# Layer norms of a two-block network: moved onto token rows on VectorE, ahead of the TensorE transposes

## The chip, the core and the metric

The kernel runs on one core of one Trainium2 chip. The metric is the device time of one launch in microseconds (us); a run is compared by the median over several launches.

## What is computed

One launch runs two transformer-like blocks on 512 tokens of width 1024, in fp32. The first ends in a mixture of experts (MoE) and a norm by `final_g`. The second has two layers, and it holds five layer norms: one at its entry, two in each layer.

```python
def layer_norm(x, g, b):
    xf = x.astype(jnp.float32)
    mu = jnp.mean(xf, -1, keepdims=True)
    var = jnp.mean(jnp.square(xf - mu), -1, keepdims=True)
    return ((xf - mu) * lax.rsqrt(var + LN_EPS) * g.astype(jnp.float32) + b.astype(jnp.float32)).astype(x.dtype)

def second_block(x, ...):
    x = layer_norm(x, ln_in_g, ln_in_b)
    for l in range(DEPTH_2):
        proj = jnp.einsum('bsd,de->bse', x, w_in[l])
        ...
        mix = jnp.einsum('bse,ed->bsd', merged, w_out[l])
        x = layer_norm(DN_ALPHA * x + mix, ln1_g[l], ln1_b[l])
        gu = jnp.einsum('bsd,df->bsf', x, w_ffn_in[l])
        hidden = jax.nn.silu(gu[..., :D_FF]) * gu[..., D_FF:]
        ffn = jnp.einsum('bsf,fd->bsd', hidden, w_ffn_out[l])
        x = layer_norm(DN_ALPHA * x + ffn, ln2_g[l], ln2_b[l])
    return x
```

## The kernel before

The 512 tokens are four tiles of 128 rows. A product in fp32 is made of three TensorE matmuls on numbers that are split into a rounded high part and a low part: `split` (lines 138 to 140) lets ScalarE cast the high part (line 139) and VectorE subtract it from the source to get the low part (line 140); `split_sb` (lines 142 to 144) does both on VectorE. Weights are split the same way after they are loaded: their tiles are called `raw` (as loaded), `wh` and `wl` (128 x 1024, sometimes narrower). `mmk` (lines 289 to 295) issues the three matmuls.

A matmul wants its activations with the features on the partitions, so between a layer norm and the next product the token rows have to be transposed. `normalizer` (line 1216) makes the function `norm` for one of the five norms; `turn` inside it is the transposition. For one tile of 128 rows the kernel before does this:

- VectorE collects mean and variance (`bn_stats`, `bn_aggr`), ScalarE takes a reciprocal root (`rsqrt`, line 185), VectorE refines it with three operations on 128 x 1 (lines 190 to 192) and makes the shift -mean * r (line 246).
- ScalarE applies scale and shift to the whole row (line 1232, 128 x 1024, in place).
- TensorE transposes the eight 128 x 128 pieces into two PSUM banks called `xt`, four to a bank (line 1246).
- For each piece ScalarE applies gain and bias, which are now per partition, from PSUM into an SBUF tile `xs` (line 1249), casts it into the high half of a page `xT` (line 139), and VectorE subtracts to make the low half (line 140).
- GpSimd applies the gain row `gR` (`lng` in the profile) and the bias row `bR` (`lnb`) to the token rows (lines 1251 and 1252, 128 x 1024 each), which SyncE's queue (SP) then stores for the residual of the next stage (line 1253).

The last norm of the second layer needs no transposition. There ScalarE does scale and shift in two halves of 512 (line 1227), GpSimd applies gain and bias for the first three tiles and VectorE for the last one (lines 1228 and 1229), and each half is stored at once (line 1230).

The five norms will be called stages: A is the one at the entry of the second block (after the MoE, loop from line 1940), B and C are the first and second norm of layer 0, D the first of layer 1, E the last. In B to E the function `residual` (line 1893) runs the product ahead of the norm in two halves of 512 columns; at the end of the second half VectorE adds each tile's PSUM result to the residual (`ev`, line 1905), and the norm follows. `lagging` puts off each `turn` by one tile. After B and D the product with `w_ffn_in` follows (TensorE results called `fm`), after A and C the projection `nav`. The order of the instructions on each engine is set by the framework's scheduler from the program; PSUM has three banks for transposes.

`row` (line 977) loads a 1024-wide vector onto all partitions by a DMA of 512 KB on SP's queue; the gain and bias rows of stage A are asked for behind the last expert weights (`w2r`, line 1403). `columns` (line 165) gathers per-partition vectors by small DMAs on ScalarE's queue and one transpose.

Of the kernel before, what the change touches and what calls it, by code (L numbers as in the profile page):

```python
# [14 lines left out]
AF = mybir.ActivationFunctionType  # L15
OP = mybir.AluOpType
# [48 lines left out]
def build(ctx, tc, I, out, dbg=None):  # L65
    nc = tc.nc
    V, S, G, PE = nc.vector, nc.scalar, nc.gpsimd, nc.tensor
# [8 lines left out]
    def t_(shape, dt, tag, name):  # L76
        uid[0] += 1
        return sb.tile(shape, dt, tag=tag, bufs=NB[tag], name=f"{name}_{uid[0]}")

    def pg(name, dt=F32R, shape=(128, 2, 512)):  # L80
        return t_(list(shape), dt, "PG", name)
# [34 lines left out]
    def sg(name, w=512, dt=F32):  # L116
        return t_([128, w], dt, "SG", name)
# [4 lines left out]
    def sm(name, w, dt=F32):  # L122
        return t_([128, w], dt, "SM", name)
# [5 lines left out]
    def trp(name):  # L129
        return mmp(name, "tr")  # L130

    def const(name, shape, dt=F32):
        return cp.tile(list(shape), dt, name=name)

    def f(ap):
        return ap.bitcast(F32)

    def split(hi, lo, src, eng=None):
        S.copy(hi, src)  # L139
        (eng or V).tensor_tensor(lo, src, f(hi), OP.subtract)  # L140

    def split_sb(hi, lo, src):
# [10 lines left out]
    R1 = [("norm1_g", I["norm1_g"][0], 8), ("b_mod", I["b_mod"][0, 0:2048], 16),  # L153
          ("conv_w", I["conv_w"][0], 40), ("conv_b", I["conv_b"][0], 10), ("b_rg_a", I["b_rg_a"][0], 10),
          ("b_rg_x", I["b_rg_x"][0], 10), ("lam", I["lru_lambda"][0], 10), ("kvg", I["kv_norm_g"][0], 2)]
    R2 = [("ln_in_g", I["ln_in_g_2"], 8), ("ln_in_b", I["ln_in_b_2"], 8), ("ln1_g", I["ln1_g_2"], 16),
          ("ln1_b", I["ln1_b_2"], 16), ("ln2_g", I["ln2_g_2"][0], 8), ("ln2_b", I["ln2_b_2"][0], 8),
          ("b_gate", I["b_gate_2"], 48), ("subln", I["diff_subln_g_2"], 2), ("qng", I["mla_q_norm_g_2"], 6),
          ("kvng", I["mla_kv_norm_g_2"], 4)]
    col = {}  # L160

# [3 lines left out]
    def columns(specs, tag):  # L165
        rows = t_([128, 128], F32, "SG", f"rows{tag}")
        n = 0
        for name, ap, k in specs:
            src = ap.rearrange("(k p) -> k p", p=128) if len(ap.shape) == 1 else \
                ap.rearrange("a (k p) -> (a k) p", p=128)  # L170
            nc.scalar.dma_start(rows[n:n + k, :], src)
            n += k
        ps = trp(f"rowst{tag}")
        PE.transpose(ps[:, 0:n], rows[0:n, :], ident[0:n, 0:n])
        cols = const(f"cols{tag}", [128, n])
        V.tensor_copy(cols, ps[:, 0:n])
        n = 0
        for name, ap, k in specs:
            col[name] = cols[:, n:n + k]
            n += k  # L180
# [1 line left out]
    columns(R0, "0")  # L182


    def rsqrt(v, n):

        y = sm("rsy", n)
        S.activation(y, v, AF.Abs_reciprocal_sqrt)
        t = sm("rst", n)
        V.tensor_tensor(t, y, y, OP.mult)  # L190
        V.scalar_tensor_tensor(t, t, -0.5, v, OP.mult, OP.mult)
        V.scalar_tensor_tensor(t, t, 1.5, y, OP.add, OP.mult)
        return t
# [48 lines left out]
    def ln_stat(mv, v):  # L242

        r = rsqrt(v, 1)
        nm = sm("bnm", 1)
        V.scalar_tensor_tensor(nm, mv[:, 0:1], -1.0, r, OP.mult, OP.mult)
        return r, nm
# [566 lines left out]

    columns(R2, "2")
    rope8 = const("rope8", [128, 2, 4, 8])
# [145 lines left out]
    for d in range(8):  # L962
# [3 lines left out]
        v = sg("mv")  # L966
# [10 lines left out]
    def row(name, src, pinned=False):  # L977
        t = pg(name, F32, (128, 1024))
        ins = load(t, src.partition_broadcast(128))
        if pinned:  # L980
            tc.keep_in_program_order(ins)
        return t
# [230 lines left out]
            V.tensor_tensor(payg[:, :, j, 32 * n:32 * n + 32], oh[:, :, j], bc(f(val)[:, :, j], 32), OP.mult)  # L1213
    gates0()

    def normalizer(gcol, bcol, gvec, bvec, dst):

        gR = row("lng", gvec, True)
        bR = row("lnb", bvec, True)
        pages = []  # L1220

        def norm(i, v, mv, var, later=None):
            r, nm = ln_stat(mv, var)
            if gcol is None:
                eng = V if i == 3 else G
                for cs in (slice(0, 512), slice(512, 1024)):
                    S.activation(v[:, cs], v[:, cs], AF.Identity, bias=nm, scale=r)
                    eng.tensor_tensor(v[:, cs], v[:, cs], gR[:, cs], OP.mult)
                    eng.tensor_tensor(v[:, cs], v[:, cs], bR[:, cs], OP.add)
                    load(dst(i)[:, :, cs], v[:, cs])  # L1230
                return
            S.activation(v, v, AF.Identity, bias=nm, scale=r)
            if later is None:
                turn(i, v)
            else:
                later.append(lambda: turn(i, v))

        def turn(i, v):
            if not pages:
                pages.extend(pg("xT") for _ in range(8))  # L1240
            tk = slice(i * 128, (i + 1) * 128)
            for q in range(2):
                b = trp("xt")
                s = sg("xs")
                for k in range(4):
                    PE.transpose(b[:, k * 128:(k + 1) * 128], v[:, (4 * q + k) * 128:(4 * q + k + 1) * 128], ident)
                for k in range(4):
                    kk, c = 4 * q + k, slice(k * 128, k * 128 + 128)
                    S.activation(s[:, c], b[:, c], AF.Identity, bias=bcol[:, kk:kk + 1], scale=gcol[:, kk:kk + 1])
                    split(pages[kk][:, 0, tk], pages[kk][:, 1, tk], s[:, c])  # L1250
            G.tensor_tensor(v, v, gR, OP.mult)
            G.tensor_tensor(v, v, bR, OP.add)
            load(dst(i), v)

        return norm, pages
# [6 lines left out]
    def rows_of(t):  # L1262
        return lambda i: t[i * 128:(i + 1) * 128, :]
# [100 lines left out]
    def pair_tokens(j):  # L1364
        xg = xgs[j % NG]
        xT = pt_("xx", F32, (128, 8, 128))
        cols = xg.rearrange("p (a j) -> p j a", j=8)
        for q in range(2):
            b = trp("xgt")
            for k in range(4):  # L1370
                PE.transpose(b[:, k * 128:(k + 1) * 128], cols[:, 4 * q + k], ident)
            (V.tensor_copy if q else S.copy)(xT[:, 4 * q:4 * q + 4].rearrange("p k n -> p (k n)"), b)
        return xT
# [6 lines left out]
    def pair_in(j, xT, beside):  # L1380
        pss = []
        for nm in ("moe_w1", "moe_w3"):
            W = [I[nm][0, 2 * j + h].rearrange("(p a) n -> p a n", a=8) for h in range(2)]
            ps = mmp("e1")
            for q in range(4):
                ws = []
                for h in range(2):
                    raw = t_([128, 2, 512], F32, ("PG", "PG", "WH", "WL")[q], "w13")
                    load(raw, W[h][:, 2 * q:2 * q + 2])
                    ws.append(raw)  # L1390
                for k in range(2):
                    both(ps, xT[:, 2 * q + k], [w[:, k] for w in ws], q + k == 0, q + k == 4)
                next(beside, None)
            pss.append(ps)
        return hidden(*pss)
# [25 lines left out]
    def nav_weights(l):  # L1421
        return TM(8, I["w_in_2"][l], 1024, 512, "nav", lead=3)

    g2R = row("g2R", mod_d[3])
    xres = [dr.tile([512, 1024], F32, name=f"xres{n}") for n in range(4)]
# [27 lines left out]
    beside = iter(())  # L1453
# [4 lines left out]
    xs = pair_tokens(0)  # L1458
    for j in range(17):
        hd = None  # L1460
        if j < 16:
            hd = pair_in(j, xs, beside)
        if j < 15:
            xs = pair_tokens(j + 1)
        if j < 14:
            pair_gather(j + 2)
        if j == 16:
            fgR = row("fgR", I["final_g"])
            nav_tm = nav_weights(0).prepare()
        if prev is not None:  # L1470
            for _ in beside:
                pass
            beside = pair_out(j - 1, prev, pair_loads(j - 1))
        prev = hd
# [39 lines left out]
    def layer(l, xT, nav_tm, x_in, x_mid, x_out):  # L1514
# [378 lines left out]
        def residual(xs, W, src, name, norm, nxt=None):  # L1893
# [18 lines left out]
                lagging(tm.run(xs, ev, nxt if hf else None), later)  # L1912
            return tm.next

        norm, xT = normalizer(col["ln1_g"][:, 8 * l:8 * l + 8], col["ln1_b"][:, 8 * l:8 * l + 8], I["ln1_g_2"][l], I["ln1_b_2"][l], rows_of(x_mid))
        residual(mT, I["w_out_2"][l], x_in, "mix2", norm)


# [4 lines left out]
        for j in range(22):  # L1923
            pgt = first.pop(0) if j < 2 else fgt.tile(128 * j)
            s = sg("ffs")
# [4 lines left out]
            p = (pg if j < 16 else pt_)("hid")  # L1930
            split_sb(p[:, 0], p[:, 1], s)
            hid.append(p)
        norm, xT = normalizer(*((col["ln2_g"], col["ln2_b"]) if l == 0 else (None, None)), I["ln2_g_2"][l], I["ln2_b_2"][l], x_out)
        if l == 0:
            return xT, residual(hid, I["w_ffn_out_2"][l], x_mid, "ffo", norm, nxt=lambda: nav_weights(1))
        residual(hid, I["w_ffn_out_2"][l], x_mid, "ffo", norm)

    lat0 = {}
    norm, xT = normalizer(col["ln_in_g"], col["ln_in_b"], I["ln_in_g_2"], I["ln_in_b_2"], rows_of(xres[0]))
    for i in range(4):  # L1940
        a = h1t[i]

# [4 lines left out]
        mv = bn(a, 1024)  # L1947
        v = sm("msq", 1)
# [3 lines left out]
    xT, nav_tm = layer(0, xT, nav_tm, xres[0], xres[1], rows_of(xres[2]))  # L1952
# [32 lines left out]
```

## Time and profile before

| | before |
|---|---|
| median of 3 runs | 3204.37 us (3203.67 to 3213.02) |
| the profiled execution | 3206.89 us |
| its span in the trace | 3205.0 us |
| mean granted TensorE clock | 0.976 of full speed |
| TensorE matmuls (PE) | 2981.3 us, 93% of the span |
| VectorE (DVE) | 1871.9 us, 58% |
| ScalarE (ACT) | 1197.2 us, 37% |
| GpSimd (POOL) | 374.9 us, 12% |

The profile was taken on one execution, whose own time is 1.89 us above its span: that is what lies around the first and last instruction. Busy times add up what an engine works; for an engine that waits for another inside an instruction, the instruction is shown longer. Where a row ends in brackets, they hold the idle time of that engine just before, and what ended it.

### The profile page before, as it was taken

What the parts mean: (1) busy time and instruction counts of PE and PEld (TensorE: products, weight loads), DVE (VectorE), ACT (ScalarE), POOL (GpSimd) and SP (SyncE); (2) the same over time, 40 slices, a digit from 0 to 9 for tenths busy, and PEclk for the clock granted to TensorE, in tenths of its full rate; (3) what the DMA queues carried; (4) which work ended last, traced back from release to release, by engine and by line L of the source; (5) the groups of instructions that cost most, each with busy time, mean ns of one, the idle gap of its engine ahead of it and who ended that gap; (6) DMA issues with size and microseconds to landing.
All of it is one profiled execution on the core that took longest, in us unless ns stands there. A gap on an engine that the chain in (4) does not pass through costs nothing.

```text
span 3205.0 us, 36688 instructions
## 1 busy us (share of the span) xinstructions
PE 2981.3 (93%) x13749; PEld 2213.1 (69%) x13749; DVE 1871.9 (58%) x3485; ACT 1197.2 (37%) x2138; POOL 374.9 (12%) x307
## 2 busy tenths in 40 slices
PE   6988999879999997999999899998999999989998
PEld 5766777733333335888877788887878876778886
DVE  6799887633332337554689744435554589764434
ACT  4555343200000015444567432224444577442222
POOL 2133000200000003111001300002211000220001
PEclk9989999989999998999999999999999999999999
DMA  6232755679999993342234532342433234622342
GB/s 218 91 96 81 235 191 187 219 282 362 377 364 367 377 374 97 125 128 92 71 112 137 193 103 89 105 138 99 144 112 103 68 107 116 220 92 92 105 138 59
DMA packets 296385, 534.21 MB, mean 167 GB/s; under 512 B 30342, under 2 KB 172916, under 8 KB 296198
## 3 DMA queue, kind: packets, MB, share of 16 engines
q1 hardware_dynamic: 293480, 527.46, 47.8%
q0 software_dynamic: 2304, 4.20, 0.5%
q8 instruction: 110, 1.80, 0.2%
q14 instruction: 77, 0.63, 0.1%
q10 hardware_dynamic: 414, 0.12, 0.0%
HBM read 486.54 MB, written 44.38 MB: 166 GB/s over the span
## 4 chain that ended last, share of the span: by engine, by line
PE 63%; DVE 8%; issue 3%; ACT 3%; DMA 1%; POOL 1%; SPq 0%; POOLq 0%; DVEq 0%; ACTq 0%
PE e L1378 12%; PE fm L292 9%; PE fm L295 9%; PE fm L293 9%; PE ffo L295 2%; PE ffo L293 2%; PE ffo L292 2%; DVE xT L140 2%; PE cmb L1308 1%; PE cmb L1309 1%; DVE wl L140 1%; POOL tl L1640 1%; PE mix L292 1%; PE mix L295 1%; PE mix L293 1%
## 5 line engine op out<-in xcount | busy, mean ns | idle before, releaser
L140 DVE TENSOR_TENSOR wl<-raw,wh 128x1024 fp32r<-128x1024 f32 (+3 forms) x403 | 467.8, 1162 | 316.6 <-ACT wh L139 315.3
L139 ACT CAST wh<-raw 128x1024 fp32r<-128x1024 f32 (+3 forms) x403 | 388.7, 966 | 545.4 <-PE fm L295 226.0
L293 PE MATMUL fm<-xT,wl 128*128 128x512 f32 (+1 forms) x1264 | 483.1, 384 | 9.6 <-DVE wl L140 9.6
L292 PE MATMUL fm<-xT,wh 128*128 128x512 f32 (+1 forms) x1264 | 485.0, 386 | 6.0 <-DVE xT L140 3.5
L295 PE MATMUL fm<-xT,wh 128*128 128x512 f32 (+1 forms) x1264 | 302.6, 382 | 0.0
L1378 PE MATMUL e<-w,xx 128*64 128x512 f32 x1024 | 293.7, 605 | 0.0
L293 PEld LDWEIGHTS fm<-xT,wl 128*128 128x128 f32 x1264 | 240.8, 190 | 55.7 <-DVE wl L140 10.6
L292 PEld LDWEIGHTS fm<-xT,wh 128*128 128x128 f32 x1264 | 240.6, 190 | 52.0 <-DVE xT L140 3.9
L295 PEld LDWEIGHTS fm<-xT,wh 128*128 128x128 f32 x1264 | 232.5, 189 | 45.5
L1378 PEld LDWEIGHTS e<-w,xx 128*64 128x64 f32 x1024 | 78.7, 137 | 139.0 <-issue 131.1
L1310 DVE TENSOR_TENSOR h<-h,cmb 128x512 f32<-128x512 f32 x128 | 84.7, 685 | 109.3 <-PE cmb L1309 108.6
L293 PE MATMUL fm<-uT,wl 128*128 128x512 f32 (+1 forms) x360 | 143.9, 400 | 3.8 <-DVE wl L140 3.8
L292 PE MATMUL fm<-uT,wh 128*128 128x512 f32 (+1 forms) x360 | 143.4, 399 | 0.0
L1378 PE MATMUL e<-w2r,hp 128*64 128x512 f32 x512 | 138.7, 599 | 2.0 <-ACT hp L1413 2.0
L292 PE MATMUL ffo<-wl,hid 128*128 128x512 f32 x352 | 137.1, 390 | 0.0
L293 PE MATMUL ffo<-wh,hid 128*128 128x512 f32 x352 | 136.9, 389 | 0.0
L1640 POOL TENSOR_TENSOR tl<-ml,tl 128x512 f32<-128x512 f32 x32 | 47.7, 1497 | 555.1 <-DVE tl L1636 550.4
L1378 PEld LDWEIGHTS e<-w2r,hp 128*64 128x64 f32 x512 | 52.9, 136 | 82.9 <-issue 63.2
L1927 DVE SCALAR_TENSOR_TENSOR ffs<-ffs,fm 128x512 f32<-128x512 f32 x44 | 30.2, 687 | 134.2 <-ACT ffs L1926 134.2
L295 PE MATMUL ffo<-wh,hid 128*128 128x512 f32 x352 | 108.4, 389 | 0.0
L139 ACT CAST yh<-y 128x512 fp32r<-128x512 f32 x32 | 19.8, 618 | 222.3 <-DVE y L1299 222.3
L140 DVE TENSOR_TENSOR xT<-xs,xT 128x128 fp32r<-128x128 f32 x128 | 86.2, 718 | 23.8 <-ACT xT L139 23.8
(612 smaller groups left out, 6101.2 us busy)
## 6 DMA issues: line engine op xcount, KB each, us to landing
w<-in_moe_w_dram SPq DMA_DIRECT2D x256, 512.0 KB
raw<-in_w_in_dram SPq DMA_DIRECT2D x71, 1024.0 KB
w2r<-in_moe_w_dram SPq DMA_DIRECT2D x128, 512.0 KB
raw<-in_w_ffn_in_dram SPq DMA_DIRECT2D x44, 1024.0 KB
raw<-in_w_mod_dram SPq DMA_DIRECT2D x42, 512.0 KB
raw<-in_w_ffn_out_dram SPq DMA_DIRECT2D x20, 1024.0 KB
raw<-in_w_out_dram SPq DMA_DIRECT2D x12, 1024.0 KB
t_d<-bg SPq DMA_DIRECT2D x48, 256.0 KB
```

The source lines that it names most:

```text
L139: S.copy(hi, src)
L140: (eng or V).tensor_tensor(lo, src, f(hi), OP.subtract)
L292: PE.matmul(ps, l[0], r[1], start=start and n == 0, stop=False)
L293: PE.matmul(ps, l[1], r[0], start=False, stop=False)
L295: PE.matmul(ps, l[0], r[0], start=False, stop=stop and n == len(pairs) - 1)
L1308: PE.matmul(ps, pl, yl[:, cs], start=True, stop=False)
L1309: PE.matmul(ps, pl, yh[:, cs], start=False, stop=True)
L1310: V.tensor_tensor(h1[i][m], h1[i][m], ps, OP.add)
L1378: PE.matmul(ps[hs], lhs[:, hs], rhs[h], start=start, stop=stop)
L1640: G.tensor_tensor(th, m, th, OP.add)
L1927: V.scalar_tensor_tensor(s, s, 1.0, pgt, OP.add, OP.mult)
```

## The change

`norm` now works on the token rows in two VectorE passes: `(v - mean) * gR` over 128 x 1024, which is issued beside ScalarE's reciprocal root and needs no r, and then `v * r + bR` in two halves of 512. TensorE transposes the finished rows. ScalarE casts each piece straight from the PSUM bank, and VectorE subtracts straight from it too; `xs`, ScalarE's scale and shift passes (lines 1232, 1227 and 1249), the operation of line 246 and all GpSimd work of the norms are gone. The rows are stored as they are. The six vectors that were needed per partition leave the list of `columns`. The normalizer of stage A is made at the MoE's step 16, ahead of the last expert pair, so that its two row loads stand elsewhere in SP's queue.

```diff
-    R2 = [("ln_in_g", I["ln_in_g_2"], 8), ("ln_in_b", I["ln_in_b_2"], 8), ("ln1_g", I["ln1_g_2"], 16),
-          ("ln1_b", I["ln1_b_2"], 16), ("ln2_g", I["ln2_g_2"][0], 8), ("ln2_b", I["ln2_b_2"][0], 8),
-          ("b_gate", I["b_gate_2"], 48), ("subln", I["diff_subln_g_2"], 2), ("qng", I["mla_q_norm_g_2"], 6),
+    R2 = [("b_gate", I["b_gate_2"], 48), ("subln", I["diff_subln_g_2"], 2), ("qng", I["mla_q_norm_g_2"], 6),
...
-    def rsqrt(v, n):
+    def rsqrt(v, n, beside=None):
         y = sm("rsy", n)
         S.activation(y, v, AF.Abs_reciprocal_sqrt)
+        if beside:
+            beside()
...
         def norm(i, v, mv, var, later=None):
-            r, nm = ln_stat(mv, var)
-            if gcol is None:
-                eng = V if i == 3 else G
-                for cs in (slice(0, 512), slice(512, 1024)):
-                    S.activation(v[:, cs], v[:, cs], AF.Identity, bias=nm, scale=r)
-                    eng.tensor_tensor(v[:, cs], v[:, cs], gR[:, cs], OP.mult)
-                    eng.tensor_tensor(v[:, cs], v[:, cs], bR[:, cs], OP.add)
+            r = rsqrt(var, 1, lambda: V.scalar_tensor_tensor(v, v, mv[:, 0:1], gR, OP.subtract, OP.mult))
+            for cs in (slice(0, 512), slice(512, 1024)):
+                V.scalar_tensor_tensor(v[:, cs], v[:, cs], r, bR[:, cs], OP.mult, OP.add)
+                if not paged:
                     load(dst(i)[:, :, cs], v[:, cs])
+            if not paged:
                 return
-            S.activation(v, v, AF.Identity, bias=nm, scale=r)
...
                 b = trp("xt")
-                s = sg("xs")
...
-                    S.activation(s[:, c], b[:, c], AF.Identity, bias=bcol[:, kk:kk + 1], scale=gcol[:, kk:kk + 1])
-                    split(pages[kk][:, 0, tk], pages[kk][:, 1, tk], s[:, c])
-            G.tensor_tensor(v, v, gR, OP.mult)
-            G.tensor_tensor(v, v, bR, OP.add)
+                    split(pages[kk][:, 0, tk], pages[kk][:, 1, tk], b[:, c])
             load(dst(i), v)
...
         if j == 16:
             fgR = row("fgR", I["final_g"])
+            norm, xT = normalizer(I["ln_in_g_2"], I["ln_in_b_2"], rows_of(xres[0]))
             nav_tm = nav_weights(0).prepare()
```

How the instructions stand now. First ScalarE in stage B, from the first tile's reciprocal root (`rsy`) on; names end in a number that tells one buffer from another, and what an instruction waits for stands in brackets. Before:

```order
L188 ACTIVATE rsy_15022<-bvr_15020 128x1 [waits DVE_49]
L1232 ACTIVATE res_14831<-res_14831,bnm_15028,rst_15024 128x1024 [waits DMAHW4_49,DVE_49]
L1249 ACTIVATE xs_15080<-xt_15079,cols_2957 128x128 [waits PE_49]
L1249 ACTIVATE xs_15080<-xt_15079,cols_2957 128x128
L139 CAST xT_15071<-xs_15080 128x128 [waits Activation_49]
L139 CAST xT_15072<-xs_15080 128x128 [waits Activation_49]
L1249 ACTIVATE xs_15080<-xt_15079,cols_2957 128x128
L188 ACTIVATE rsy_15062<-bvr_15060 128x1 [waits DVE_49]
L1249 ACTIVATE xs_15080<-xt_15079,cols_2957 128x128
```

And with the change:

```order
L186 ACTIVATE rsy_14968<-bvr_14966 128x1 [waits DVE_49]
L139 CAST xT_15017<-xt_15025 128x128 [waits PE_49]
L139 CAST xT_15018<-xt_15025 128x128 [waits DVE_49]
L139 CAST xT_15019<-xt_15025 128x128 [waits DVE_49]
L186 ACTIVATE rsy_15008<-bvr_15006 128x1 [waits DVE_49]
L139 CAST xT_15020<-xt_15025 128x128 [waits DVE_49]
L139 CAST xT_15021<-xt_15038 128x128 [waits PE_49]
L139 CAST xT_15022<-xt_15038 128x128 [waits DVE_49]
L139 CAST xT_15023<-xt_15038 128x128 [waits DVE_49]
L139 CAST xT_15017<-xt_15092 128x128 [waits PE_49]
L139 CAST xT_15021<-xt_15105 128x128 [waits PE_49]
```

The passes of lines 1232 and 1249 are gone; a cast that is not the first of its bank now waits for VectorE (DVE), where it waited only for ScalarE itself before.

VectorE at the same place with the change, for the second tile (`res_14779`), from the addition of its residual to the end of its norm:

```order
L1899 SCALAR_TENSOR_TENSOR res_14779<-res_14779,mix_3209_14977 128x512 [waits PE_49]
L140 TENSOR_TENSOR xT_15017<-xt_15025,xT_15017 128x128 [waits Activation_49]
L216 BN_STATS bst_14909<-res_14779 128x6 [waits DVE_49]
L140 TENSOR_TENSOR xT_15018<-xt_15025,xT_15018 128x128 [waits Activation_49]
L221 BN_AGGR bmv_15004<-bst_14909 128x2 [waits DVE_49]
L1252 TENSOR_SCALAR bvr_15006<-bmv_15004 128x1 [waits DVE_49]
L1223 SCALAR_TENSOR_TENSOR res_14779<-res_14779,bmv_15004,lng_14773 128x1024
L190 TENSOR_TENSOR rst_15011<-rsy_15008 128x1 [waits Activation_49]
L140 TENSOR_TENSOR xT_15019<-xt_15025,xT_15019 128x128
L191 SCALAR_TENSOR_TENSOR rst_15011<-rst_15011,bvr_15006 128x1 [waits DVE_49]
L192 SCALAR_TENSOR_TENSOR rst_15011<-rst_15011,rsy_15008 128x1 [waits DVE_49]
L1225 SCALAR_TENSOR_TENSOR res_14779<-res_14779,rst_15011,lnb_14775 128x512 [waits DVE_49]
```

The two row passes (lines 1223 and 1225) stand among the subtractions of the tile before (line 140), which read the PSUM bank `xt` instead of `xs`.

SP's queue ahead of the last expert pair, with the change (the eight `w2r` loads that follow are shown by their first):

```order
L979 DMA fgR_9345<-in_final_g_dram 128x1024
L979 DMA lng_9347<-in_ln_in_g_dram 128x1024
L979 DMA lnb_9349<-in_ln_in_b_dram 128x1024
L393 DMA raw_9351<-in_w_in_dram 128x4x512
L393 DMA raw_9353<-in_w_in_dram 128x4x512
L1396 DMA w2r_9399<-in_moe_w_dram 128x1024
```

`lng` and `lnb` stood behind the eighth `w2r` load before; now both `raw` loads and all eight `w2r` loads come after them.

## Rows read from the trace of the kernel before

**Rows 1.** Windows, stages A to E: us, busy of PE, PEld, DVE, ACT, POOL, granted clock, DMA share, GB/s.

```profile
1209.40:1262.90 53.50, 35.27 (x128) 26.11 (x129) 41.68 (x79) 31.30 (x84) 21.56 (x10) 0.81 0.18 64
1810.30:1863.00 52.70, 40.44 (x249) 35.78 (x248) 37.22 (x72) 30.00 (x79) 19.81 (x8) 0.90 0.19 70
2189.60:2244.80 55.20, 45.98 (x202) 36.73 (x201) 38.77 (x73) 31.14 (x81) 20.26 (x8) 0.91 0.27 91
2796.10:2848.80 52.70, 40.64 (x249) 36.11 (x249) 37.26 (x72) 30.07 (x79) 19.58 (x8) 0.90 0.19 71
3175.40:3205.00 29.60, 16.27 (x72) 13.14 (x70) 17.77 (x36) 6.89 (x12) 15.26 (x12) 0.84 0.27 71
```

**Rows 2.** VectorE beside GpSimd in stage B: timeline (start us, us, engine, line, operation).

```profile
1819.24 2.39 POOL L1252 TENSOR_TENSOR res<-res,lnb 128x1024 f32<-128x1024 f32 x1
1819.30 2.48 DVE L140 TENSOR_TENSOR xT<-xs,xT 128x128 fp32r<-128x128 f32 x1
1821.70 0.15 DVE L190 TENSOR_TENSOR rst<-rsy 128x1 f32<-128x1 f32 x1
```

**Rows 3.** The subtractions of all norm stages, by tile: duration ns min/median/max.

```profile
L140 DVE TENSOR_TENSOR xT<-xs,xT x128: 229/282/2520, 1217.0 to 2838.3; 128x128 fp32r<-128x128 f32 x128
```

**Rows 4.** The path through stage B: timeline; the last row is the next stage's first.

```profile
1811.07 0.69 DVE L216 BATCH_NORM_STATS2 bst<-res 128x6 f32<-128x512 f32 x1
...
1833.01 1.20 PE L1246 MATMUL xt<-ident,res 128*128 128x128 f32 x8 [2.68 <-ACT res L1232]
...
1837.44 2.83 DVE L140 TENSOR_TENSOR wl<-raw,wh 128x1024 fp32r<-128x1024 f32 x1
...
1840.33 0.58 PE L293 MATMUL fm<-xT,wl 128*128 128x256 f32 x1 [4.31 <-DVE wl L140]
...
1849.13 3.67 DVE L140 TENSOR_TENSOR xT<-xs,xT 128x128 fp32r<-128x128 f32 x7
...
1863.02 0.40 PE L292 MATMUL fm<-xT,wh 128*128 128x512 f32 x1
```

**Rows 5.** Groups of VectorE instructions by shape: busy us, mean ns of one, idle before.

```profile
L140 DVE TENSOR_TENSOR wl<-raw,wh 128x1024 fp32r<-128x1024 f32 x314 | 391.9, 1249 | 299.3 <-ACT wh L139 298.4 <-PE idx L321 0.5
L795 DVE SCALAR_TENSOR_TENSOR macc<-raw,csil,macc 128x1024 f32<-128x1024 f32 x28 | 36.0, 1287 | 5.3 <-DMA raw<-in_w_mod_dram 5.3
L1059 DVE SCALAR_TENSOR_TENSOR u<-u,rst,sh2R 128x512 f32<-128x512 f32 x8 | 5.6, 746 | 0.1
```

**Rows 6.** The end of stage A on VectorE: timeline.

```profile
1250.17 5.62 DVE L140 TENSOR_TENSOR xT<-xs,xT 128x128 fp32r<-128x128 f32 x8 [4.97 <-ACT xT L139]
```

**Rows 7.** The last tile of stage E: timeline.

```profile
3191.71 0.69 DVE L1905 SCALAR_TENSOR_TENSOR res<-res,ffo 128x512 f32<-128x512 f32 x1 [0.62 <-PE ffo L295]
...
3193.59 0.20 ACT L188 ACTIVATE rsy<-bvr 128x1 f32<-128x1 f32 x1 [0.95 <-DVE bvr L1259]
3193.83 0.81 DVE L190 TENSOR_TENSOR rst<-rsy 128x1 f32<-128x1 f32 x1 [0.27 <-ACT rsy L188]
...
3200.14 0.69 DVE L1229 TENSOR_TENSOR res<-res,lnb 128x512 f32<-128x512 f32 x1
```

**Rows 8.** Groups of ScalarE instructions by shape: columns as in rows 5.

```profile
L1249 ACT ACTIVATE xs<-xt,cols 128x128 f32<-128x128 f32 x128 | 53.4, 462 | 14.0 <-PE xt L1246 14.0
L139 ACT CAST xT<-xs 128x128 fp32r<-128x128 f32 x128 | 32.5, 305 | 0.1
```

**Rows 9.** SP's queue at the MoE's end (timeline), and transfers meanwhile (windows, columns as rows 1).

```profile
1191.12 0.33 SPq L979 DMA_DIRECT2D lng<-in_ln_in_g_dram  x1
...
1191.00:1199.00 8.00, 5.44 (x26) 2.48 (x28) 4.16 (x6) 0.62 (x2) 0.00 (x0) 1.00 1.03 409
```

**Rows 10.** TensorE's granted clock in the middle of stage B: windows, columns as rows 1.

```profile
1833.00:1844.00 11.00, 5.45 (x26) 4.81 (x27) 8.98 (x19) 7.49 (x24) 4.75 (x2) 0.54 0.12 49
```

**Rows 11.** VectorE at 128 x 512, source in PSUM and source in SBUF: groups, columns as rows 5.

```profile
L1310 DVE TENSOR_TENSOR h<-h,cmb 128x512 f32<-128x512 f32 x128 | 84.7, 685 | 109.3 <-PE cmb L1309 108.6
L144 DVE TENSOR_TENSOR hid<-ffs,hid 128x512 fp32r<-128x512 f32 x44 | 30.1, 684 | 0.0
```

More of the change, by code (lines that the diff above doesn't have):

```diff
@@ L1214, in build, with normalizer @@
     gates0()
-    def normalizer(gcol, bcol, gvec, bvec, dst):
+    def normalizer(gvec, bvec, dst, paged=True):
         gR = row("lng", gvec, True)
@@ L1913, in residual @@
             return tm.next
-        norm, xT = normalizer(col["ln1_g"][:, 8 * l:8 * l + 8], col["ln1_b"][:, 8 * l:8 * l + 8], I["ln1_g_2"][l], I["ln1_b_2"][l], rows_of(x_mid))
+        norm, xT = normalizer(I["ln1_g_2"][l], I["ln1_b_2"][l], rows_of(x_mid))
         residual(mT, I["w_out_2"][l], x_in, "mix2", norm)
@@ L1932, in layer @@
             hid.append(p)
-        norm, xT = normalizer(*((col["ln2_g"], col["ln2_b"]) if l == 0 else (None, None)), I["ln2_g_2"][l], I["ln2_b_2"][l], x_out)
+        norm, xT = normalizer(I["ln2_g_2"][l], I["ln2_b_2"][l], x_out, l == 0)
         if l == 0:
@@ L1938, in build @@
     lat0 = {}
-    norm, xT = normalizer(col["ln_in_g"], col["ln_in_b"], I["ln_in_g_2"], I["ln_in_b_2"], rows_of(xres[0]))
     for i in range(4):
```

## The prediction

> **What bounds the kernel now.** I read the windows of the five norm stages first, then inside one stage the timeline and the waits, then the groups by shape for durations, and last the order of the instructions with the change. TensorE is busy 93% of the span, so only a stage where it idles can give anything. The stages are such places: in A to D it works 35.27, 40.44, 45.98 and 40.64 us of 53.50, 52.70, 55.20 and 52.70 [rows 1], so 18.2, 12.3, 9.2 and 12.1 us are idle, 51.8 us together. A 3205 us kernel has little more than that to win here, plus the tail of E and what the low clock costs.
>
> Why it idles: in stage B TensorE waits 2.68 us for ScalarE's pass over the whole row, and later 4.31 us for VectorE to finish a weight's low half, which took 2.83 us itself [rows 4], against a mean of 1.249 [rows 5]. The reader is to see why it took so long. A subtraction of 128 x 128 starts at 1819.30, 0.06 us after a GpSimd pass, and ends at 1821.78, 0.15 us after that pass ends [rows 2]; half of all such subtractions take under 0.282 us, the longest 2.52 [rows 3]. In E an operation on 128 x 1 takes 0.81 us [rows 7], where another takes 0.15 [rows 2]. So VectorE stands still while GpSimd works on rows. [...]
>
> **What the change costs and gives.** GpSimd's passes go. So do ScalarE's pass over the row and its 8 gain and bias passes per tile (0.462 us each [rows 8]). VectorE gets one pass of 128 x 1024 and two of 128 x 512 per tile. The nearest rows with the same form (tile, per-partition number, second tile in SBUF) are 1.287 us for the wide one and 0.746 for the narrow [rows 5]: 2.78 us per tile, 55.6 us for twenty tiles. This is new work on the engine that the stages wait for. It is covered only if it is less than the standstill that goes.
>
> Stage B: VectorE now has per tile the residual's addition 0.69 [rows 7], one statistics pass 0.69 [rows 4], five small operations at 0.15 to 0.2 (0.8), the passes 1.287 + 2 x 0.746, and eight subtractions at 0.282: 7.2 us. Four tiles are 28.9, and three weight subtractions at 1.249 that stand among them make 32.6. From 1810.30 [rows 1] this ends at 1842.9. Before, the last subtraction ended at 1849.13 + 3.67 = 1852.80 [rows 4]; the next stage began 10.2 us later, which is TensorE work that stays. So B gives 9.9 us. D has the same window [rows 1] and the same order: 9.9. C is the same chain, but TensorE idles only 9.2 us there [rows 1]: 9.0.
>
> Stage A has on VectorE the multiplication by `final_g` (1.287) in place of the residual's addition, a second statistics pass and one more small operation: 8.7 us per tile, 34.6 for four, 38.4 with the weights. From 1209.40 it ends at 1247.8, where the last subtraction ended at 1255.79 [rows 6]: 8.0 us. Before, the three weights stood behind that point in the order and now they stand ahead of it, which is another 3.7 for TensorE's next product: 11.5, taken a little low.
>
> Stage E: from 3191.71 the last tile needs 0.69 + 0.69 + 0.3 + 1.287 + 0.45 + 1.49 = 4.9 us to 3196.6, where it was done at 3200.83 [rows 7]. The store behind it (4.2 us to the span's end) stays: 4.2. The five sum to 44.5 us.
>
> Against this stand two new things. **Turns on a bank.** In the order every cast after the first of a bank waits for VectorE, which it did not before: ScalarE casts piece k+1 of a PSUM bank only after VectorE has subtracted piece k. No row shows such a pair. From below it costs nothing: while VectorE is at its row passes (2.78 us and the small operations per tile) ScalarE runs ahead, and two banks can alternate. From above, each piece takes a cast 0.305 [rows 8], a subtraction 0.282 [rows 3] and two hand-overs of 0.07 together (VectorE idles 0.27 around a ScalarE operation of 0.20 [rows 7]): 0.657 in place of 0.282, so 0.375 per piece, 3.0 per tile, 12 per stage, 48 in all. I take 2 us per stage, 8 in all, near the lower end, because in the order the row passes of the next tile stand between the subtractions of three tiles in four and the last tile's pieces alternate between its banks. [...]
>
> **The row loads of A.** They move ahead of two `raw` and eight `w2r` loads on SP's queue. 2 x 512 KB at the 409 GB/s of [rows 9] is 2.6 us by which the last expert weights could come later; the DMA share is 1.03 there, so nothing absorbs it but slack in TensorE's own order. Bounds 0 and 2.6; I take 1.3. The rows themselves now land early, which nobody waits for. Six small DMAs on ScalarE's queue go early in the program, far from any stage: nothing.
>
> VectorE now reads the pieces from PSUM. At 128 x 512 it took 0.685 us with a source in PSUM and 0.684 with sources in SBUF only [rows 11], so I charge nothing. [...]
>
> Sum: 44.5 - 8 - 1.3 = 35.2 us. The profiled execution took 3206.89, its span 3205.0; 3206.89 - 35.2 = 3171.7. The median of the runs is 2.5 us below the profiled one, so **3169 us**, 1.1% faster. (About 0.3%, 9.6 us, can be told from no change here.)
>
> **Rivals.**
> 1. The turns are all hidden and the loads cost nothing: 44.5 us, or 3160. If TensorE in addition never waits in A to D, 51.8 + 4.2 = 56 us, or 3148. For it: the clock of 0.54 [rows 10] would come back with the waits, and no step above counts that. Against: VectorE's 7.2 us per tile are real, and TensorE still waits for the first tile. Chance 0.16.
> 2. Half the pieces pay the full turn: 24 us in place of 8, so 44.5 - 24 - 2.6 = 18 us, or 3186. For it: the first tile of each stage has one bank behind the other in the order, and ScalarE's next reciprocal root stands behind casts that wait. Chance 0.13.
> 3. Slower: ScalarE and VectorE alternate with nothing in between, 0.375 us for each of the 128 pieces, 48 us, with 2.6 for the loads: 44.5 - 50.6 = -6, or 3210.5. It decides from 0.34 us per piece. Past that, with the stages longer, TensorE would keep the low clock of [rows 10] in the 10.2 us that follow the last subtraction; 4 us in each of the four stages would make it 3226. Against: 2.78 us of row passes per tile lie beside the casts. Chance 0.05, of which 0.02 past 0.3%.
> 4. The change doesn't do what it says: the long subtractions are not GpSimd's doing but the trace's account of some other wait. Then VectorE keeps them and gets 55.6 us of passes, with ScalarE's 2.68 us waits gone: within 10 us of before either way. [Rows 2] speak against it. Chance 0.02, half of it slower.
>
> **How the numbers follow.** The forecast has the remaining 0.64. The range must hold 8 in 10: the forecast's own range, with the turns at 4 to 16 us and the loads at 0 to 2.6, is 3164 to 3178; half of rival 1 and most of rival 2 come in with 3153 to 3188. Left out are the far end of rival 1, the slow part of rival 2, and rivals 3 and 4. Faster by over 0.3%: forecast, rivals 1 and 2, 0.93. Slower: 0.02 + 0.01, 0.03. Between: 0.04.
>
> **What would show it.** In the changed profile GpSimd has no busy time in the five stages; the subtractions have a longest of under 0.5 us and a median near 0.28; the two new passes take 1.29 and 0.75 us. B and D last about 45 us, C 48, A 43, E 25.5. Busy VectorE and idle ScalarE in the stages confirm the pace; idle VectorE that ends on a cast (line 139) shows turns, and their sum over A to D is to be near 8 us. The last expert matmuls end within 2.6 us of where they did. I am wrong if the subtractions stay long without GpSimd, if VectorE idles some 20 us or more on casts, or if the stages shorten and TensorE's clock stays at 0.54 in them.

## The result, and the profile after

The changed kernel takes 3159.99 us in the median of 6 runs (3154.16 to 3160.60). The kernel before, run beside it, took 3210.42 (3203.67 to 3213.28, 6 runs). The ratio is 0.9842, with a 95% interval of 0.9827 to 0.9856: 1.58% faster, about 50 us. The profiled execution took 3154.16 us, its span is 3152.4; before it was 3206.89 and 3205.0.

The five stages of the changed kernel, as windows with the columns of [rows 1]:

```profile
1212.90:1252.00 39.10, 30.77 (x128) 22.80 (x129) 35.03 (x87) 16.22 (x48) 0.00 (x0) 0.91 0.25 87
1800.90:1841.20 40.30, 37.85 (x248) 34.11 (x248) 31.21 (x80) 15.17 (x43) 0.00 (x0) 1.00 0.25 93
2167.80:2211.30 43.50, 42.63 (x201) 34.47 (x201) 33.39 (x81) 16.24 (x45) 0.00 (x0) 1.00 0.34 116
2760.00:2800.40 40.40, 37.96 (x250) 34.21 (x249) 31.25 (x80) 15.16 (x43) 0.00 (x0) 1.00 0.25 93
3127.00:3152.40 25.40, 16.27 (x72) 13.14 (x70) 18.95 (x40) 0.81 (x4) 0.00 (x0) 0.86 0.28 83
```

Against [rows 1], A is 14.4 us shorter, B 12.4, C 11.7, D 12.3 and E 4.2: 55 us. GpSimd (the fifth busy time) has no work in them. TensorE idles 8.3, 2.5, 0.9 and 2.4 us in A to D, where it idled 18.2, 12.3, 9.2 and 12.1, and in B, C and D it is granted its full clock (1.00) where it had 0.90, 0.91 and 0.90. Its busy time in C fell from 45.98 to 42.63 us for the same matmuls. Of the 55 us, 2.5 do not reach the end: stage A starts 3.6 us later in this execution, and the stretches A to B and C to D differ by +1.5 and -2.5 us.

The casts and subtractions by tile, with durations in ns as min/median/max (before: [rows 3]):

```profile
L139 ACT CAST xT<-xt x128: 253/266/272, 1219.9 to 2789.1; 128x128 fp32r<-128x128 f32 x128
L140 DVE TENSOR_TENSOR xT<-xt,xT x128: 234/282/294, 1220.4 to 2789.4; 128x128 fp32r<-128x128 f32 x128
```

The longest subtraction is 294 ns where it was 2520, and the median is 282 ns as before, although the source is now in PSUM. No surcharge for that source shows, as [rows 11] had said.

The path through stage B, from the timeline:

```profile
1800.93 0.69 DVE L1899 SCALAR_TENSOR_TENSOR res<-res,mix 128x512 f32<-128x512 f32 x1 [2.38 <-PE mix L295]
...
1802.69 1.28 DVE L1223 SCALAR_TENSOR_TENSOR res<-res,bmv,lng 128x1024 f32<-128x1024 f32 x1
1803.89 0.15 DVE L190 TENSOR_TENSOR rst<-rsy 128x1 f32<-128x1 f32 x1
...
1811.59 0.48 DVE L140 TENSOR_TENSOR xT<-xt,xT 128x128 fp32r<-128x128 f32 x2
1812.40 0.29 DVE L140 TENSOR_TENSOR xT<-xt,xT 128x128 fp32r<-128x128 f32 x1 [0.33 <-ACT xT L139]
...
1824.72 0.66 PE L1242 MATMUL xt<-ident,res 128*128 128x128 f32 x4 [1.61 <-DVE res L1225]
...
1827.05 0.68 DVE L140 TENSOR_TENSOR xT<-xt,xT 128x128 fp32r<-128x128 f32 x3
...
1827.19 0.39 PE L293 MATMUL fm<-xT,wl 128*128 128x256 f32 x1 [0.63 <-DVE wl L140]
...
1830.22 0.29 DVE L140 TENSOR_TENSOR xT<-xt,xT 128x128 fp32r<-128x128 f32 x1 [0.33 <-ACT xT L139]
...
1841.20 0.40 PE L292 MATMUL fm<-xT,wh 128*128 128x512 f32 x1
```

The waits of 2.68 and 4.31 us of [rows 4] are 1.61 and 0.63 here, both behind VectorE. The last subtraction ends at 1830.51, 29.6 us after the stage's first instruction; before it was 42.5 (1852.80 less 1810.30). From there to the next stage it is 10.7 us, before 10.2. So the whole gain of B lies ahead of the last subtraction.

The end of stage E, timeline:

```profile
3143.31 0.69 DVE L1899 SCALAR_TENSOR_TENSOR res<-res,ffo 128x512 f32<-128x512 f32 x1 [0.48 <-PE ffo L295]
...
3146.84 1.41 DVE L1225 SCALAR_TENSOR_TENSOR res<-res,rst,lnb 128x512 f32<-128x512 f32 x2
```

The last tile is done 4.94 us after its addition began (9.1 before, [rows 7]), and the span ends 4.15 us later.

### The profile page after: what moved, and what is told of

Its sections match the earlier page's. It is cut to its first block, busy times and chain, and to the rows that moved or that the text cites. A ratio compares the mean times of both kernels' runs of the same rounds, so it can differ in the third digit from the quotient of the medians.

```text
span 3152.4 us, 36476 instructions
## 1 busy us (share of the span) xinstructions
PE 2970.1 (94%) x13749; PEld 2204.3 (70%) x13749; DVE 1848.6 (59%) x3521; ACT 1131.5 (36%) x1986; POOL 279.6 (9%) x263
## 4 chain that ended last, share of the span: by engine, by line
PE 64%; DVE 7%; issue 3%; DMA 2%; ACT 2%; POOL 1%; SPq 0%; DVEq 0%; POOLq 0%; ACTq 0%
PE e L1371 12%; PE fm L292 9%; PE fm L295 9%; PE fm L293 9%; PE ffo L295 2%; PE ffo L293 2%; PE ffo L292 2%; PE cmb L1301 1%; PE cmb L1302 1%; POOL tl L1634 1%; DVE xT L140 1%; DMA w2r<-in_moe_w_dram 1%; PE mix L292 1%; PE mix L295 1%; PE mix L293 1%
## 5 line engine op out<-in xcount | busy, mean ns | idle before, releaser
L1921 DVE SCALAR_TENSOR_TENSOR ffs<-ffs,fm 128x512 f32<-128x512 f32 x44 | 30.3, 688 | 137.7 <-ACT ffs L1920 137.7
L1923 DVE SCALAR_TENSOR_TENSOR ffs<-ffs,fm 128x512 f32<-128x512 f32 x44 | 30.3, 688 | 114.4 <-PE fm L295 114.4
```

The lines of the kernel that those rows point to most:

```text
L1921: V.scalar_tensor_tensor(s, s, 1.0, pgt, OP.add, OP.mult)
L1923: V.scalar_tensor_tensor(s, s, 0.5, pup, OP.mult, OP.mult)
```

## The experiments

All stage lengths go from VectorE's first instruction of the stage to TensorE's first of the next, and E's to the span's end:

| us | A | B | C | D | E | median of runs |
|---|---|---|---|---|---|---|
| before | 53.6 | 52.7 | 55.1 | 52.7 | 29.6 | 3210.42 |
| changed | 39.1 | 40.3 | 43.4 | 40.3 | 25.4 | 3159.99 |
| changed, run again | 39.1 | 40.3 | 43.5 | 40.3 | 25.4 | 3154.79 |
| GpSimd's passes to VectorE, rest as before | 43.9 | 42.8 | 44.5 | 41.0 | 29.7 | 3171.34 |
| changed, GpSimd's passes into scratch | 47.3 | 48.9 | 56.6 | 48.9 | 25.4 | 3196.99 |
| changed, GpSimd's passes in place | 47.0 | 51.6 | 54.9 | 50.7 | 25.3 | 3196.74 |
| changed, casts of a bank first | 40.7 | 38.3 | 41.7 | 38.3 | 25.4 | 3153.24 |
| the same in B, C and D only | 39.1 | 38.3 | 41.8 | 38.3 | 25.4 | 3150.36 |
| changed, one more VectorE pass | 43.1 | 46.2 | 50.9 | 46.1 | 27.7 | 3181.27 |

The stage lengths repeat within 0.1 us in the two profiles of the changed kernel. A third profile, of the run with the row loads back (last experiment below), has the same VectorE instructions in the same order in B to E, and there D took longer. Its window:

```profile
2759.20:2801.00 41.80, 39.35 (x249) 35.62 (x248) 31.26 (x80) 15.14 (x43) 0.00 (x0) 0.96 0.24 89
```

TensorE idles 2.4 us in it as in the changed kernel, and the last subtraction comes after the same 29.6 us; the granted clock is 0.96 in place of 1.00. So a stage with the same instructions can differ by 1.5 us, with the clock as the only difference in these numbers. The medians of the changed kernel differ by 5 us between the two sets of runs, so small effects are read from the stages and from runs of one set.

### GpSimd's passes added to the changed kernel

```diff
+            w = pt_("gw", F32, (128, 1024))
+            G.tensor_tensor(w, v, gR, OP.mult)
+            G.tensor_tensor(w, w, bR, OP.add)
             load(dst(i), v)
```

> The changed kernel with two GpSimd passes of 128 x 1024 per tile added to stages A to D, which read the finished rows and write a scratch tile that nobody uses; VectorE, ScalarE and TensorE keep their work and, but for a handful of neighbours that swap, their order. Theory 1 (GpSimd's passes hold VectorE back): the subtractions of 128 x 128 again have a longest of over 2 us, GpSimd is busy some 20 us in each of the four stages, each of them is 7 to 13 us longer than the changed kernel's 39, 40, 43 and 40 us, and the whole is 28 to 50 us slower than the changed kernel (3185 to 3210). Rival (the gain came from ScalarE's passes, which are still gone): the subtractions stay under 0.3 us and the whole within 5 us of the changed kernel, 3155 to 3165.

Measured: 3196.99 us (3194.83 to 3198.66), ratio 0.9953 (0.9938 to 0.9968), 37 to 42 us slower than the changed kernel. The time came as theory 1 said, the means did not: it had the subtractions long again, and they are not. VectorE, by tile and in the timeline of stage B:

```profile
L140 DVE TENSOR_TENSOR xT<-xt,xT x128: 236/281/293, 1223.4 to 2833.7; 128x128 fp32r<-128x128 f32 x128
```

```profile
1820.56 2.35 DVE L190 TENSOR_TENSOR rst<-rsy 128x1 f32<-128x1 f32 x1
...
1827.68 3.25 DVE L1223 SCALAR_TENSOR_TENSOR res<-res,bmv,lng 128x1024 f32<-128x1024 f32 x1
...
1833.30 3.26 DVE L140 TENSOR_TENSOR wl<-raw,wh 128x1024 fp32r<-128x1024 f32 x1
```

What is held are operations with two operands in SBUF, down to 128 x 1: 2.35, 3.25 and 3.26 us in these rows, where the changed kernel has 0.15 and 1.28 for the first two and a mean of 1.23 for its weight subtractions of that shape. A subtraction that takes one tile from PSUM goes through: 83 of the 128 ran beside a GpSimd pass, and the longest took 293 ns. So does a statistics pass, which reads one tile (0.69 us at most beside a GpSimd pass). The scratch tiles came from a pool that is full in C, which delayed GpSimd there (its first pass waits for a matmul of `ffo` until 15.2 us into the stage, in the next run until 6.4), so the passes were put back in place as well:

```diff
+            G.tensor_tensor(v, v, gR, OP.mult)
+            G.tensor_tensor(v, v, bR, OP.add)
             load(dst(i), v)
```

> The changed kernel with the two GpSimd passes of the kernel before put back at their old place (times gR, plus bR, in place on the rows, ahead of the store), in stages A to D; the rows that are stored, and with them the later residuals, get gain and bias twice. VectorE, ScalarE and TensorE have the changed kernel's instructions in the changed kernel's order. In the earlier run the passes wrote scratch tiles of a pool that is still full in stage C; here they need none. Theory 1, as the earlier run corrected it (GpSimd's pass holds VectorE's operations with two SBUF operands: the passes, the weights' low halves, the operations on 128 x 1; the subtractions, which read one operand from PSUM, pass): subtractions under 0.3 us, single operations of those other kinds over 2 us, A, B and D 7 to 10 us longer than the changed kernel, C 7 to 12, the whole 28 to 42 us slower. Rival (a large part of the 42 us of the earlier run came from waiting for scratch tiles): at most 15 us slower in all.

Measured: 3196.74 us (3194.62 to 3201.99), ratio 0.9961 (0.9950 to 0.9973), 42 us slower than the changed kernel's second set. A is 7.9 us longer, B 11.3, C 11.4, D 10.4: theory 1, a little over its bounds in B and D. Stage B, timeline:

```profile
1815.51 2.36 DVE L1223 SCALAR_TENSOR_TENSOR res<-res,bmv,lng 128x1024 f32<-128x1024 f32 x1
1816.86 3.25 POOL L1247 TENSOR_TENSOR res<-res,lnb 128x1024 f32<-128x1024 f32 x1
1817.79 2.34 DVE L190 TENSOR_TENSOR rst<-rsy 128x1 f32<-128x1 f32 x1
1820.06 0.28 DVE L140 TENSOR_TENSOR xT<-xt,xT 128x128 fp32r<-128x128 f32 x1
```

A 128 x 1 operation starts inside a GpSimd pass and ends when that ends (1820.13 and 1820.11). GpSimd is held as well: its second pass takes 3.25 us against 2.39 in [rows 2]. With the same instructions in the same order on the three other engines, this is the price of GpSimd's passes alone: some 41 of the 50 us.

### GpSimd's passes to VectorE, the rest as before

```diff
-            G.tensor_tensor(v, v, gR, OP.mult)
-            G.tensor_tensor(v, v, bR, OP.add)
+            V.tensor_tensor(v, v, gR, OP.mult)
+            V.tensor_tensor(v, v, bR, OP.add)
```

> The kernel before with one edit: the two row passes of stages A to D (lines 1251 and 1252) run on VectorE instead of GpSimd; ScalarE's passes, xs and the order of the row loads stay, stage E too. Theory 1: VectorE's standstill goes, but it gets 16 x 2 passes of 1.25 us, 10 us per stage; part of it stands beside waits for ScalarE, so each stage is 4 to 9 us shorter than before and the whole 16 to 36 us faster (ratio 0.989 to 0.995), with subtractions under 0.35 us. Rival (ScalarE's passes on the way to TensorE were what cost): no stage gets shorter by more than 2 us, and the whole is the same or slower than before.

Measured: 3171.34 us (3167.32 to 3172.01), ratio 0.9875 (0.986 to 0.989): 40 us, more than theory 1 gave it. The stages as windows:

```profile
1215.00:1258.90 43.90, 32.13 (x129) 23.82 (x129) 35.24 (x87) 31.14 (x84) 0.00 (x0) 0.88 0.22 79
1806.10:1849.00 42.90, 39.36 (x249) 35.51 (x249) 30.40 (x80) 29.91 (x79) 0.00 (x0) 0.96 0.23 85
2175.60:2220.10 44.50, 42.19 (x201) 34.47 (x200) 32.42 (x81) 30.82 (x81) 0.00 (x0) 1.00 0.33 112
2768.30:2809.30 41.00, 37.73 (x249) 33.92 (x248) 30.21 (x80) 29.77 (x79) 0.00 (x0) 1.00 0.24 90
```

ScalarE is as busy as before (30 to 31 us a stage), and of A to D all but A come within 2.6 us of the changed kernel. Eight more VectorE passes a stage cost less than the standstill that they replace: VectorE's busy time falls from 37.22 [rows 1] to 30.40 us in B. The rest of the change, ScalarE's passes with all that hangs on them, is worth 4.8, 2.5, 1.1 and 0.7 us in A to D, by the table. E keeps GpSimd's passes in this run; there the whole change is worth 4.3.

### One more VectorE pass

```diff
+            w = pt_("vw", F32, (128, 1024))
+            V.tensor_tensor(w, v, gR, OP.mult)
             r = rsqrt(var, 1, lambda: V.scalar_tensor_tensor(v, v, mv[:, 0:1], gR, OP.subtract, OP.mult))
```

> The changed kernel with one more VectorE pass of 128 x 1024 per tile in all five stages, into a scratch tile that nobody reads: 20 passes of about 1.2 us. Theory 1 (VectorE paces stages A, B and D, and nearly C, where TensorE idles under 1 us): A, B and D 3.5 to 5 us longer, C 2 to 5, E 1 to 2, the whole 13 to 21 us slower than the changed kernel. Rival (TensorE's work or the turns with ScalarE set the pace, and VectorE has room): less than 1.5 us per stage, the whole under 6 us slower.

Measured: 3197.45 us (3194.47 to 3202.72), ratio 0.9965 (0.9954 to 0.9977), 43 us slower than the changed kernel beside it, far over both. A (43.6 us) is as theory 1 has it, B (46.6) and D (46.3) are about 1 us over its bounds; C took 60.0 and E 34.3. There the extra pass of the first tile stands behind the additions of the second and third in the order, and VectorE waits for those. Timeline of C:

```profile
2177.50 0.16 DVE L192 SCALAR_TENSOR_TENSOR rst<-rst,rsy 128x1 f32<-128x1 f32 x1
2180.43 0.69 DVE L1901 SCALAR_TENSOR_TENSOR res<-res,ffo 128x512 f32<-128x512 f32 x1 [2.77 <-PE ffo L295]
```

The scratch tile comes from a pool that the operands of that product (`hid`) fill, by the code. That is a fault of the experiment, so it was made again in place:

```diff
+            V.tensor_tensor(v, v, v, OP.max)
             r = rsqrt(var, 1, lambda: V.scalar_tensor_tensor(v, v, mv[:, 0:1], gR, OP.subtract, OP.mult))
```

> The changed kernel with one more VectorE pass of 128 x 1024 per tile in all five stages, in place and without a scratch tile (the maximum of a row with itself). The earlier run took its scratch tiles from a pool that is full in C and E, and lost 16 and 9 us there with waits for it. Theory 1 (VectorE paces A, B and D, and nearly C): A, B and D 4 to 6 us longer than the changed kernel, as in the earlier run, C 3 to 6, E 1 to 3, the whole 16 to 26 us slower. Rival (C is bound by TensorE): C under 2 us longer.

Measured: 3181.27 us (3179.16 to 3182.01), ratio 0.9911 (0.9889 to 0.9934), 26 us slower than the changed kernel's second set. The added passes by shape (busy us, mean ns):

```profile
L1223 DVE TENSOR_TENSOR res<-res 128x1024 f32<-128x1024 f32 x16 | 18.7, 1172 | 0.0
L1223 DVE TENSOR_TENSOR h<-h 128x1024 f32<-128x1024 f32 x4 | 4.9, 1217 | 0.0
```

23.6 us of passes cost 25.4 us of stages, so VectorE has no room for them; but it is not one for one. A lost 4.0 us for 4.9 us of passes and E 2.3 for 4.7; B, C and D lost 5.9, 7.4 and 5.8 us for 4.7 each. Stage B as a window, and TensorE's wait for the last tile's rows in it:

```profile
1805.80:1852.00 46.20, 39.65 (x249) 35.60 (x248) 34.99 (x84) 15.04 (x43) 0.00 (x0) 0.93 0.22 81
```

```profile
1831.77 1.98 PE L1243 MATMUL xt<-ident,res 128*128 128x128 f32 x8 [5.38 <-DVE res L1226]
```

The last subtraction ends 32.4 us after the stage's first instruction, 2.8 later than in the changed kernel (29.6); the rest of the four passes went into VectorE's waits (1.7 us there, 0.8 here) and into the overlap of neighbouring instructions. The other 3.1 us come behind the last subtraction: TensorE waited 5.38 us where it waited 1.61, and worked on at a clock of 0.93 in the stage against 1.00. In C, too, the last subtraction comes only 2.8 us later. TensorE's idle time there went from 0.9 to 6.8 us, its clock from 1.00 back to 0.93 and its busy time from 42.65 to 44.06 us in the windows of the stage; that is more than theory 1 gave.

### The turns on a PSUM bank

```diff
                 for k in range(4):
-                    kk, c = 4 * q + k, slice(k * 128, k * 128 + 128)
-                    split(pages[kk][:, 0, tk], pages[kk][:, 1, tk], b[:, c])
+                    S.copy(pages[4 * q + k][:, 0, tk], b[:, k * 128:k * 128 + 128])
+                for k in range(4):
+                    p = pages[4 * q + k]
+                    V.tensor_tensor(p[:, 1, tk], b[:, k * 128:k * 128 + 128], f(p[:, 0, tk]), OP.subtract)
```

> The changed kernel with ScalarE's four casts of a PSUM bank written first and VectorE's four subtractions of it after them, so that the two engines take one turn per bank instead of four; same operations, same numbers. Theory 1 (the turns are nearly hidden, as VectorE idles only 3 us on casts in the changed trace): A, B and D shorter by 0 to 1 us each, C unchanged since TensorE idles under 1 us there, the whole 0 to 4 us faster than the changed kernel. Rival (turns cost the 8 us that the forecast took): 6 to 10 us faster.

Measured: 3153.24 us (3148.32 to 3155.89), ratio 0.9819 (0.9806 to 0.9833). B, C and D are 1.9, 1.8 and 2.0 us shorter, A 1.7 us longer: between the two theories, and the 3 us that VectorE idles on casts were no bound. In C, where the same weight subtractions stand ahead of the last subtraction, that comes 1.3 us earlier: VectorE idles 0.4 us less, and neighbouring instructions overlap by 0.7 us more. In A TensorE's transposes of the third and fourth tile wait 1.67 and 1.65 us for VectorE's rows, 0.38 us each in the changed kernel. Then only in B, C and D:

```diff
-    def normalizer(gvec, bvec, dst, paged=True):
+    def normalizer(gvec, bvec, dst, paged=True, turns=False):
...
+                if turns:
+                    for p, s in part:
+                        split(p[:, 0, tk], p[:, 1, tk], s)
+                else:
+                    for p, s in part:
+                        S.copy(p[:, 0, tk], s)
+                    for p, s in part:
+                        V.tensor_tensor(p[:, 1, tk], s, f(p[:, 0, tk]), OP.subtract)
...
-            norm, xT = normalizer(I["ln_in_g_2"], I["ln_in_b_2"], rows_of(xres[0]))
+            norm, xT = normalizer(I["ln_in_g_2"], I["ln_in_b_2"], rows_of(xres[0]), turns=True)
```

> As the run with the casts of a bank first, but in stages B, C and D only; stage A keeps the order of the changed kernel. Theory 1 (the turns cost about 2 us in each of B, C and D, as the earlier run showed with 38.4, 41.7 and 38.3 us against 40.3, 43.4 and 40.3; and stage A's 1.7 us loss in that run came from its new order): A at 39 us, B and D at 38.3, C at 41.7, the whole 5 to 7 us faster than the changed kernel beside it. Rival (those differences are what two executions differ by): stages within 0.5 us of the changed kernel's beside it, the whole within 2 us.

> The changed kernel again, as the one that the others of this set are compared with on the same chip. Both theories: 0.982 to 0.986 of the kernel before.

Measured: 3150.36 us (3147.05 to 3151.01), ratio 0.9813 (0.9796 to 0.9831); beside it the changed kernel took 3154.79 (3153.00 to 3155.07), ratio 0.9829 (0.9812 to 0.9846). The two do not overlap: 4.4 us faster, a little under the 5 to 7 expected, and A is back at 39.1. B, C and D as windows:

```profile
1802.00:1840.30 38.30, 37.46 (x249) 34.06 (x248) 30.45 (x80) 13.54 (x43) 0.00 (x0) 1.00 0.26 96
2166.90:2208.70 41.80, 41.80 (x201) 34.62 (x200) 32.54 (x81) 14.60 (x45) 0.00 (x0) 1.00 0.35 119
2758.30:2796.60 38.30, 37.47 (x249) 34.06 (x248) 30.46 (x80) 13.54 (x43) 0.00 (x0) 1.00 0.26 97
```

TensorE idles 0.8, 0.0 and 0.8 us: TensorE's waits have nothing more to give in these three stages. This version beats both kernels.

### The row loads of stage A

```diff
-            norm, xT = normalizer(I["ln_in_g_2"], I["ln_in_b_2"], rows_of(xres[0]))
             nav_tm = nav_weights(0).prepare()
...
     lat0 = {}
+    norm, xT = normalizer(I["ln_in_g_2"], I["ln_in_b_2"], rows_of(xres[0]))
```

> The changed kernel with the normalizer of stage A made where it was before, so that its two row loads stand behind the last expert weights again. Theory 1 (the moved loads push the last expert weights back by 2 to 2.6 us): the last expert matmuls do not wait for w2r, and stage A starts 1.5 to 2.5 us earlier in its trace against the MoE's milestones; the whole is about 2 us faster than the changed kernel. Rival (the 3.6 us by which stage A starts later come from elsewhere): no change within 1 us; or the rows now come too late for the first norm and it is slower by 1 to 3 us.

The second run has this edit together with the casts first in B, C and D:

> Casts of a bank first in B, C and D, and the row loads of stage A behind the last expert weights as in the kernel before. Theory 1 (the moved loads cost the last expert weights about 2 us): 1 to 3 us faster than the run with the casts first in B, C and D alone, ratio 0.980 to 0.981. Rival (the end of the MoE differs by that much from execution to execution, and the place of the two loads does not show): within 1.5 us of it.

Measured: 3155.33 us (3152.59 to 3159.62), ratio 0.9825 (0.9812 to 0.9839), where the changed kernel had 0.9842 and 0.9829; and with the casts first in B, C and D 3150.36 us (3144.34 to 3151.46), ratio 0.9809 (0.9789 to 0.9829), where the same kernel without it had 0.9813. Intervals of this width can't show 2 us. The last expert matmuls in TensorE's timeline, of the changed kernel and then with the loads behind the weights (this run, the one with the casts first, and the kernel before):

```profile
1194.82 10.86 PE L1371 MATMUL e<-w2r,hp 128*64 128x512 f32 x32 [2.13 <-DMA w2r<-in_moe_w_dram]
```

```profile
1193.37 9.65 PE L1371 MATMUL e<-w2r,hp 128*64 128x512 f32 x32 [0.68 <-ACT hp L1406]
```

```profile
1196.72 8.83 PE L1377 MATMUL e<-w2r,hp 128*64 128x512 f32 x32 [0.68 <-ACT hp L1412]
```

```profile
1194.31 7.74 PE L1378 MATMUL e<-w2r,hp 128*64 128x512 f32 x32 [0.68 <-ACT hp L1413]
```

With the loads back the 2.13 us wait is gone. Counted from the end of the same earlier wait of TensorE for VectorE (at 1187.26, 1184.62, 1188.34 and 1185.93), the matmuls end 18.4, 18.4, 17.2 and 16.1 us later. So the first two executions alone would say that nothing was won, and the others say 1.2 to 2.3 us. The clock differs between them: it is 0.74, 0.81 and 1.00 in the three with the loads behind the weights, where the matmuls take 9.65, 8.83 and 7.74 us. In all eight profiles with the moved loads the end comes after 18.1 to 18.7 us, at clocks from 0.84 to 1.00; in the four with the loads behind after 16.1, 17.2, 17.2 and 18.4. On average that is 1.2 us, as theory 1 has it in direction and nearly in size. What reaches stage A is not shown: it starts 25.4 to 26.8 us after that wait with the moved loads, and 23.4, 25.1, 25.1 and 27.4 with the loads behind. Of the 3.6 us by which it starts later in the changed kernel's profile, 2.3 lie behind that wait.

## Why the prediction was right, and where its sizes were off

The forecast was 3169 us, 1.1% faster; measured were 3160 and 1.58%, within the range. That 3160 is also rival 1's first value is luck: that value stands for 44.5 us off a kernel of 3204.37 us with the turns hidden. Measured were 50 us off a kernel that took 3210.42 in these runs, and the turns were not hidden. For the same reason the time was missed by 9 us only, and the gain by 15.

**What held VectorE back.** Right. In place, with everything else in the changed kernel's order, GpSimd's two passes cost 41 us; taken off the kernel before and given to VectorE, 40. The forecast named the subtractions first as what is held. That is true of the kernel before; the changed one takes that operand from PSUM and would be spared there (294 ns at most with the passes in place), while its own row passes would be held (2.36 and 3.25 us for 1.28).

**VectorE's new passes are on the path.** Right in the sum: 23.6 us of added passes cost 25.4 us. But not pass by pass: the four added to B (4.7 us) put its last subtraction only 2.8 us later, and another 3.1 us came from TensorE's longer wait and lower clock.

**The term for B and D** (9.9 us each, less 2 for turns) measured 12.4 and 12.3. The step that failed is VectorE's sum of 32.6 us to the last subtraction: it was 29.6, with the turns in it. The sum added the rows' durations, and these came out as forecast (32.4 in B). But a row overlaps the next. The wide pass takes 1.28 us and the next instruction starts 1.20 after it; two subtractions in a group take 0.48, three 0.68, so one more costs 0.20 and not 0.282. Over the 75 instructions of B that is 4.5 us, of which VectorE's short waits for TensorE, for ScalarE and for its own results take back 1.7.

**The term for C** (9.0 us, less 2) measured 11.7. The step that failed is TensorE's idle time of 9.2 us as the bound. Of the 11.7 us, 8.3 were idle time; TensorE's own work shrank by another 3.4 us for the same matmuls, with the clock at 1.00 instead of 0.91. Rival 1 had named this clock and priced the case from the idle time alone.

**The term for A** (11.5 us, less 2) measured 14.4, for both reasons (TensorE's own work shrank by 4.5 us, with the clock at 0.91 instead of 0.81). **E** (4.2) measured 4.2.

**The turns** (2 us per stage, a choice between bounds of 0 and 12) were sized right for B, C and D: 1.8 to 2.0 us with one turn per bank. Most of what they cost does not stand in VectorE's idle time on casts, 0.7 us in B; part of it is overlap that is lost where a subtraction waits for its cast (0.7 us in C). In A the other order lost 1.7 us, with TensorE's longer waits for VectorE's rows; no run was made on it.

**The moved loads** (1.3 us): the last expert matmuls ended 1.2 us later on average, between bounds that were 0 and 2.6. What of it reaches the whole stays open: the medians can't show it.

So 35 us were forecast and some 50 came. Rival 2 (half the turns exposed), rival 3 (slower) and rival 4 (not GpSimd's doing) all fall: the last by the passes put back, the others by the turns' measured 2 us in B, C and D and by stages that all got shorter.

## What to carry to other kernels

Work on a side engine that nobody waits for can still set the pace, as GpSimd's two passes per tile did here (41 us over A to D): look for an operation on the pacing engine that takes far longer than its like and ends with the side engine's (2.34 us on 128 x 1 for 0.15, ending 0.02 us after the pass). On the pacing engine, count an operation by the start of the next and not by its row's length (1.20 and 1.28 us for the wide pass here), and add the waits. TensorE's idle time is no ceiling for what a stage can give back while its granted clock is under full: C gave 11.7 us with 9.2 idle, at a clock of 0.91.

## What was not expected of the hardware

- VectorE's subtractions with one operand in PSUM were untouched by GpSimd's passes: 293 ns at most, with 83 of the 128 beside one of 32 passes, where those of the kernel before, with both operands in SBUF, took up to 2520 [rows 3]. GpSimd's passes, for their part, were stretched from 2.4 to 3.25 us beside VectorE's wide passes.
- A wait for a transfer can hide what a low clock would cost. With the row loads ahead of the last expert weights, where transfers run at a DMA share of 1.04 (before 1.03, [rows 9]), the expert matmuls ended 18.1 to 18.7 us after the wait ahead of them at any clock from 0.84 to 1.00; without that wait they ended after 16.1 us at 1.00 and after 18.4 at 0.74.
